# A stream stage of an RWKV block rewritten without GpSimd, and the weight splits of two paths moved to VectorE

## The chip, the cores and the metric

One NeuronCore of a Trainium2 chip runs the whole program in one launch. The metric is the device time of one execution in microseconds. Engines are named as in the profile: PE is TensorE (PEld its weight loads), DVE is VectorE, ACT is ScalarE, POOL is GpSimd, SP is SyncE, which only issues DMAs here. Each engine runs its own queue of instructions in order and waits on semaphores.

## The reference, cut to what matters

Two blocks run one after the other on 512 latent tokens and 256 context tokens of width 1024. The first has an RWKV-7 layer and a differential attention layer; the second has two layers of feed-forward halves around a mixer (Fourier, latent attention, gating, pooling). The change lies in the RWKV layer, and in one choice of engine that the second block's context path shares.

```
proj = h @ w_in                                   # r, k, v, g and the low-rank inputs lw, la
mixed = u + mu * (0.5 * (prev + nxt) - u)         # centred token shift of all but g
w_raw = w0 + tanh(lw) @ w2 ; a = sigmoid(a0 + la @ a2)        # for each direction d
decay = exp(-exp(-softplus(-w_raw) - 0.5))
kk = k * k_k ; kk = kk * rsqrt(sum(kk * kk, per head) + 1e-12)
kd = k * (1 + (a - 1) * k_a)
# scan over time, forward and backward, S is 64x64 for each of 16 heads
sa = S kk ; S = S * w - sa (kk * a)^T + v kd^T ; o = S r
y = groupnorm(o) * gn_g + gn_b + (sum r * kd * r_k) * v ; y = y * silu(g) @ w_out
```

Everything is float32 in and out. Large products run as three products of fp32r halves: high x high, high x low, low x high.

## The kernel before, in words

The 16 heads are handled in 8 pairs j of 128 features; tokens lie along the free dimension, context first (NT = 768, HALF = 384).

**Projection** (`rwkv_project`). It goes through 34 blocks of 128 output features: `l0` and `l1` (the low-rank inputs), then for each pair k, r, v and g. For a block `WStream.load` (lines 71 to 84) fetches 512 KB of weights into `wr` by an SP DMA, ScalarE copies it to `wh` rounded to fp32r (L78), and one engine subtracts to give the rest, `wl` (L81). Which engine is the parameter `lo_engines`: GpSimd for the projection and for the second block's context path, VectorE and GpSimd in turns for the latent path. TensorE then makes 24 products for each of two segments into PSUM tile `psu` (`psg` for g), ScalarE copies them to `u`, GpSimd adds the two neighbours (`sm`, L307), ScalarE scales the middle (`m`, L309), and VectorE joins both to `mx` (L314, L315). r and k stay in SBUF for the stream stage, v and g go to DRAM. Between blocks, 80 loads of modulation weights (`adaw`, three buffers) are multiplied by a small vector (`aps`).

**Stream stage** (`rwkv_streams`, `stage1(j)`). For a pair, and for each half of the tokens: squares of k, sums by head (`pc`), an inverse root in 12 small VectorE instructions (`rsqrt_cols`, lines 51 to 61, on 128x6), six products that spread it over the features (`bc`), `kap`. Then for each direction d: two LoRA products in plain float32 with 64 rows (`psw`, `psa`), tanh, a scan along the chunks (L426), a GpSimd subtraction (L427) and three exponentials (E, Ei, cs), the streams `strm` and `str` (VectorE L439 to L447, GpSimd L446, L448, L451), their way to DRAM (dS, dL), and 64x64 products `psx` masked into M (L466). After both halves, M's 96 blocks of 32x32 are regrouped through DRAM and inverted by substitution: 30 steps of a product (L485) and a sum (L486) on VectorE; products `psy` and `psz` put the inverse together.

**Scan** (`rwkv_scan`, `stage2(j)`). Groups of four chunks are prepared (`ps`, X, `psw`, `lr`, `psg`, G; masks on VectorE L607, L618, L634) and then passed through state by state (`pch`, ScalarE L683, VectorE L685 and L688). At the end of a pair the output is normalized, and GpSimd adds the bonus and multiplies by g (L729, L730).

**Order.** `stage1` is a generator: the projection runs five of its steps after each block (`s1(5)`) and lets at most one pair wait, `stage2` from the second pair on runs one step after each of its own. `C2.emit`, the context path of the second block up to its second layer, is written after the scan and its remainder (`emit2`) inside the second block. A list scheduler orders each engine's queue at build time from this order and its own costs, so that the context path's feed-forward products (`pab`, `pf` on `chi`, `clo`) fill TensorE in the scan, in the output product (`pso`) and in the differential attention (`scores`, `ptr`, `po`).

```
eng = nc.vector if self.lo[self.i % len(self.lo)] == "v" else nc.gpsimd     # line 79
eng.tensor_tensor(out=lv, in0=rv, in1=hv, op=ALU.subtract)                  # line 81
W = WStream(S, wp, ("g",), raws=2)                                          # projection
E.W = WStream(S, wp, ("g",), 512, 3, S.nc.scalar)                           # context path, in Ctx2
```

## Time and profile before

| what | us |
|---|---|
| median of 3 runs | 4411.06 |
| lowest and highest of them | 4402.58, 4414.34 |
| the profiled execution's own time | 4410.31 |
| span of its trace, first to last instruction | 4408.5 |
| VectorE busy | 2399.9 |
| GpSimd busy | 1516.9 |

The trace is one execution. A window from A to B is in microseconds from the first instruction. Busy time is the union of an engine's instructions; matmuls overlap in the pipe, so that TensorE's busy time is more than its work. PEclk is the granted share of TensorE's full clock. "X <- Y" in a view of waits means that X's engine stood idle until Y was done.

### The profile page before, as it was taken

Reading aid. Unit: us, or ns where it says so; the run is one execution under the profiler, and the core shown is the slowest. Engines: PE = TensorE matmul, PEld = TensorE weight load, DVE = VectorE, ACT = ScalarE, POOL = GpSimd, SP = SyncE. Lnnn points to the kernel's source line nnn. Section 1 sums busy time; section 2 is a strip of 40 time slices with the busy share of each in tenths; the row PEclk is TensorE's granted clock in tenths of the full one; section 3 lists DMA queues with packets and bytes.
Section 4 is the critical chain, followed back from the end, with each engine's and each line's share of the span. In section 5 each row is a group of like instructions: output and inputs, shape, how many; then the busy total and the mean of one; then the engine's idle time right before and its main releaser. Section 6 shows DMA issues by size and latency. Waiting matters only on the chain.

```text
span 4408.5 us, 70611 instructions
## 1 busy us (share of the span) xinstructions
PE 4116.0 (93%) x27478; PEld 3447.1 (78%) x27478; DVE 2399.9 (54%) x4704; ACT 1637.3 (37%) x3018; POOL 1516.9 (34%) x1200
## 2 busy tenths in 40 slices
PE   7999978899899997999898999999999999999998
PEld 5667767889768896888787888867888888867887
DVE  4677888644655435666766434554333532555434
ACT  3333333334433443444544323344222322343222
POOL 3444445355423681432333324211222222302221
PEclk9999978999999998999999999999999999999999
DMA  7775355566787663221214333311333233302332
GB/s 260 256 239 169 120 169 163 161 200 197 232 260 229 212 190 128 74 78 56 73 61 153 101 103 109 113 58 48 97 95 96 91 96 95 121 31 63 105 96 81
DMA packets 347247, 581.55 MB, mean 132 GB/s; under 512 B 96416, under 2 KB 194848, under 8 KB 345760
## 3 DMA queue, kind: packets, MB, share of 16 engines
q1 hardware_dynamic: 205984, 402.44, 28.4%
q10 hardware_dynamic: 140928, 174.58, 13.0%
q8 instruction: 217, 3.56, 0.3%
q14 instruction: 118, 0.97, 0.1%
HBM read 509.33 MB, written 67.57 MB: 131 GB/s over the span
## 4 chain that ended last, share of the span: by engine, by line
PE 70%; DVE 8%; DMA 2%; ACT 2%; issue 1%; POOL 0%; ACTq 0%; SPq 0%; DVEq 0%; POOLq 0%
PE pab L91 9%; PE pab L90 9%; PE pab L92 9%; PE pf L90 6%; PE pf L91 6%; PE pf L92 6%; PE psg L47 2%; PE pch L47 2%; PE ps L47 1%; PE psz L91 1%; PE aps L47 1%; PE pssc L47 1%; PE psz L90 1%; PE psz L92 1%; DMA adaw<-in_adaw 1%
## 5 line engine op out<-in xcount | busy, mean ns | idle before, releaser
L81 POOL TENSOR_TENSOR wl<-wr,wh 128x512 fp32r<-128x512 f32 (+3 forms) x719 | 1096.1, 1535 | 2207.3 <-ACT wh L78 1962.7
L78 ACT ACTIVATE wh<-wr 128x512 fp32r<-128x512 f32 (+3 forms) x918 | 696.5, 766 | 1476.5 <-PE pab L91 588.4
L91 PE MATMUL pab<-llo,wh 128*128 128x512 f32 (+1 forms) x1472 | 563.2, 383 | 5.2 <-DVE llo L148 5.2
L90 PE MATMUL pab<-lhi,wh 128*128 128x512 f32 (+1 forms) x1472 | 559.9, 383 | 8.2 <-ACT lhi L146 8.2
L92 PE MATMUL pab<-lhi,wl 128*128 128x512 f32 (+1 forms) x1472 | 561.7, 382 | 0.0
L90 PE MATMUL pf<-gh,wh 128*128 128x256 f32 (+1 forms) x1328 | 449.9, 342 | 31.5 <-DVE fth L1060 10.2
L91 PE MATMUL pf<-gl,wh 128*128 128x256 f32 (+1 forms) x1328 | 449.7, 340 | 3.1 <-DVE gl L158 2.8
L92 PE MATMUL pf<-gh,wl 128*128 128x256 f32 (+1 forms) x1328 | 448.6, 341 | 1.9 <-POOL wl L81 1.9
L81 DVE TENSOR_TENSOR wl<-wr,wh 128x1024 fp32r<-128x1024 f32 (+2 forms) x199 | 238.8, 1200 | 204.6 <-ACT wh L78 202.3
L90 PE MATMUL pab<-chi,wh 128*128 128x256 f32 x1056 | 310.1, 295 | 24.6 <-DVE nt L145 8.9
L90 PEld LDWEIGHTS pab<-lhi,wh 128*128 128x128 f32 x1472 | 278.7, 191 | 61.3 <-ACT lhi L146 9.5
L91 PEld LDWEIGHTS pab<-llo,wh 128*128 128x128 f32 x1472 | 280.2, 190 | 58.7 <-DVE llo L148 6.2
L92 PEld LDWEIGHTS pab<-lhi,wl 128*128 128x128 f32 x1472 | 280.3, 190 | 52.3
L92 PE MATMUL pab<-chi,wl 128*128 128x256 f32 x1056 | 307.5, 294 | 7.2 <-POOL wl L81 7.1
L90 PEld LDWEIGHTS pf<-gh,wh 128*128 128x128 f32 x1328 | 255.1, 193 | 70.5 <-ACT wh L78 15.9
L91 PE MATMUL pab<-clo,wh 128*128 128x256 f32 x1056 | 307.5, 292 | 0.0
L91 PEld LDWEIGHTS pf<-gl,wh 128*128 128x128 f32 x1328 | 257.1, 194 | 35.5 <-DVE gl L158 4.2
L92 PEld LDWEIGHTS pf<-gh,wl 128*128 128x128 f32 x1328 | 257.3, 194 | 30.3 <-POOL wl L81 2.6
L90 PEld LDWEIGHTS pab<-chi,wh 128*128 128x128 f32 x1056 | 207.6, 197 | 32.2 <-issue 15.7
L1060 DVE TENSOR_TENSOR fth<-fth,pab 128x512 f32<-128x512 f32 (+1 forms) x154 | 88.0, 572 | 265.2 <-PE pab L92 263.4
L1059 DVE SCALAR_TENSOR_TENSOR fth<-fth,pab 128x512 f32<-128x512 f32 (+1 forms) x154 | 87.7, 569 | 257.0 <-ACT fth L1058 256.8
L1034 DVE SCALAR_TENSOR_TENSOR x<-pf,lgt,x 128x512 f32<-128x512 f32 (+1 forms) x144 | 98.7, 690 | 229.4 <-PE pf L92 229.1
(508 smaller groups left out, 8944.5 us busy)
## 6 DMA issues: line engine op xcount, KB each, us to landing
adaw<-in_adaw SPq DMA_DIRECT2D x192, 512.0 KB, 5.4
wr<-in_w SPq DMA_DIRECT2D x176, 512.0 KB, 3.5
wr<-in_w ACTq DMA_DIRECT2D x344, 256.0 KB, 3.1
wr<-in_w SPq DMA_DIRECT2D x96, 384.0 KB, 3.1
wr<-in_rwin SPq DMA_DIRECT2D x32, 512.0 KB, 5.0
wr<-in_w ACTq DMA_DIRECT2D x104, 128.0 KB, 2.2
dS<-strm SPq DMA_DIRECT2D x32, 384.0 KB, 2.8
dL<-str SPq DMA_DIRECT2D x32, 384.0 KB, 3.5
```

The source lines that it names most:

```text
L47: nc.tensor.matmul(out, lhsT, rhs, start=start, stop=stop)
L78: nc.scalar.activation(out=hv, in_=rv, func=AF.Copy)
L81: eng.tensor_tensor(out=lv, in0=rv, in1=hv, op=ALU.subtract)
L90: nc.tensor.matmul(ps, whi, xhi, start=first, stop=False)
L91: nc.tensor.matmul(ps, whi, xlo, start=False, stop=False)
L92: nc.tensor.matmul(ps, wlo, xhi, start=False, stop=last)
L1034: S.nc.vector.scalar_tensor_tensor(out=E.x[:, f, sl], in0=ps[:, sl], scalar=gate[:, f : f + 1], in1=E.x[:, f, sl], op0=ALU.mult, op1=ALU.add)
L1059: nc.vector.scalar_tensor_tensor(out=th, in0=th, scalar=1.0, in1=pa, op0=ALU.add, op1=ALU.mult)
L1060: nc.vector.tensor_tensor(out=th, in0=th, in1=pb, op=ALU.mult)
```

## The change

The stream stage, the projection's sums, the readout's sums and the weight splits of two paths no longer use GpSimd.

- *Projection.* ScalarE copies `psu` to `u` already scaled by half of mu; VectorE adds the two neighbours (L310 after) and then joins `psu`, straight from PSUM, scaled by 1 - mu (L311 after): two instructions of VectorE for each segment in place of one of VectorE for each and two for the block on GpSimd and ScalarE. `wl` is made by VectorE. r and k go to DRAM like v, and `stage1(j)` loads them. There are two `u` tiles in place of three, and two buffers for `adaw` in place of three. After each block run seven steps of the stage, and no pair is waited for; `s1.ready(j)` makes sure that pair j's stage is written before its scan, and every scan step from the first pair on runs one step of it.
- *Stream stage.* The inverse root is made once for a pair (128x12), spread by a ScalarE copy (`wide`) and six transposes. The LoRA products are two fp32r products of 128 rows each: the low-rank input is kept as tiles `tw` whose upper and lower halves of partitions are its high and its low half, against weights `lh` and `ll` that stand twice. The exponential of the exclusive sum is read from E itself, shifted by one column in a tile of 65 columns per chunk, so that L427 and one exponential are gone. The products of L446, L448, L451 and L468 are VectorE's; the scaling of L444 is ScalarE's; the inverse's transposed copy (L491) is ScalarE's.
- *Readout.* The bonus, the scale and the product with g are three VectorE forms.
- *Context path.* `wl` is made by VectorE.

In the diff below, `S.ada_bufs` is 2 in the projection and 7 elsewhere, and `S1P` is 7. The diff, cut to its core:

```diff
@@ ada
+    bufs = min(bufs, S.ada_bufs)
@@ rwkv_project
-        NU = 3
+        NU = 2
-        W = WStream(S, wp, ("g",), raws=2)
+        W = WStream(S, wp, raws=2)
-            if o[0] == "k":
-                while len(pending) > 1:
-                    s1(1)
...
-                    nc.scalar.activation(out=u[:, c : c + n], in_=ps[:, :n], func=AF.Copy)
-                nc.gpsimd.tensor_tensor(out=sm, in0=u[:, 0 : NT + 1], in1=u[:, 2 : NT + 3], op=ALU.add)
-                nc.scalar.activation(out=m1, in_=u[:, 1 : NT + 2], func=AF.Identity, scale=omu[:, mc : mc + 1])
-                nc.vector.scalar_tensor_tensor(out=mx[:, 0:NCTX], in0=sm[:, 0:NCTX], scalar=hmu[:, mc : mc + 1], in1=m1[:, 0:NCTX], op0=ALU.mult, op1=ALU.add)
-                nc.vector.scalar_tensor_tensor(out=mx[:, NCTX:], in0=sm[:, NCTX + 1 :], scalar=hmu[:, mc : mc + 1], in1=m1[:, NCTX + 1 :], op0=ALU.mult, op1=ALU.add)
+                    nc.scalar.activation(out=u[:, c : c + n], in_=ps[:, :n], func=AF.Identity, scale=hmu[:, mc : mc + 1])
+                    nc.vector.tensor_tensor(out=mx[:, sl], in0=u[:, c - 1 : c - 1 + n], in1=u[:, c + 1 : c + 1 + n], op=ALU.add)
+                    nc.vector.scalar_tensor_tensor(out=mx[:, sl], in0=ps[:, :n], scalar=omu[:, mc : mc + 1], in1=mx[:, sl], op0=ALU.mult, op1=ALU.add)
...
-            s1(5)
+            s1(S1P) 
@@ stage1
+        nc.sync.dma_start(k_, S.d_rkvg[1, j])
+        nc.sync.dma_start(r_, S.d_rkvg[0, j])
...
+        rsqrt_cols(S, rc, pc[:, 0:12], 12, 1.0, 1e-12, sp)
+        nc.scalar.activation(out=wide.rearrange("p (n r) -> p n r", r=64), in_=rc.unsqueeze(2).to_broadcast([128, 12, 64]), func=AF.Copy)
...
-                    mm(nc, ps[:, :HALF], lw[ip, d, :], tw[ip, d, hs], True, True)
+                    nc.tensor.matmul(ps[:, :HALF], lh[:, 2 * d + i, :], tw[d][i][:, hs], start=True, stop=False)
+                    nc.tensor.matmul(ps[:, :HALF], ll[:, 2 * d + i, :], tw[d][i][:, hs], start=False, stop=True)
...
-                nc.gpsimd.tensor_tensor(out=th, in0=cs, in1=th, op=ALU.subtract)
-                nc.scalar.activation(out=cs, in_=th, func=AF.Exp, scale=-0.5 * CDEC)
+                E, Ex = Es[d][:, :, 1 - d : 65 - d], Es[d][:, :, d : 64 + d]
...
-                nc.gpsimd.tensor_tensor(out=kd, in0=ta, in1=kT, op=ALU.mult)
-                nc.gpsimd.tensor_tensor(out=lr[:, 1, :], in0=rT, in1=E, op=ALU.mult)
+                nc.vector.tensor_tensor(out=kd, in0=kd, in1=kT, op=ALU.mult)
+                nc.vector.tensor_tensor(out=ch(lr[:, 1, :]), in0=ch(rT), in1=E, op=ALU.mult)
@@ rwkv_scan
+            s1.ready(j)
             for _ in stage2(j):
-                if j >= 1:
-                    s1(1)
+                s1(1)
@@ Ctx2
-        E.W = WStream(S, wp, ("g",), 512, 3, S.nc.scalar)
+        E.W = WStream(S, wp, ("v",), 512, 3, S.nc.scalar)
```

Over the whole program GpSimd goes from 1205 instructions to 474, VectorE from 4706 to 5298, ScalarE from 3852 to 3845 and TensorE from 22864 to 22880 products. Up to the projection's last product TensorE's order holds 264 of the 384 products `psx` and 96 of 192 of each inverse product before, 240 and 72 after; the last modulation load of the projection stands in block 21 of the 34 before, in block 30 after.

TensorE before, in the projection, at the LoRA products of one half of a pair (`psw` and `psa`, the decay's and the rate's low-rank products, from tile `tw`):

```order
L91 MATMUL psu<-lo,wh 128x512
L47 MATMUL psx_2207<-strm 64x64 x12
L47 MATMUL psw<-tw,lw 128x384
L92 MATMUL psu<-hi,wl 128x512
L90 MATMUL psu<-hi,wh 128x512
L91 MATMUL psu<-lo,wh 128x512
```

They are one float32 product each. The same place of TensorE's queue in the changed kernel:

```order
L47 MATMUL aps<-adaw,silc 32x256 x4
L441 MATMUL psw<-tw_474,lh 128x384
L442 MATMUL psw<-tw_474,ll 128x384
L91 MATMUL psu<-lo,wh 128x512
L92 MATMUL psu<-hi,wl 128x512
L441 MATMUL psa<-tw_475,lh 128x384
L442 MATMUL psa<-tw_475,ll 128x384
```

One float32 product became two fp32r products of the same 384 columns, and both pairs of a direction stand closer together.

VectorE before, in the projection, where a pair's inversion (L485 and L486) meets the stream stage and a block's sum `mx`:

```order
L485 TENSOR_TENSOR tmp<-B 96x30
L486 TENSOR_TENSOR B<-B,tmp 96x30
L491 COPY Bt<-B 96x1024
L410 SCALAR_TENSOR_TENSOR kap<-mx,vec,bc 128x384
L423 TENSOR_SCALAR th<-th 128x384
L426 SCALAR_TENSOR_TENSOR cs<-c_smask,th 128x384
L177 COPY adas<-aps 128x256
L439 TENSOR_TENSOR strm<-kap,cs 128x384
L441 SCALAR_TENSOR_TENSOR bb<-ta,kap 128x384
L442 SCALAR_TENSOR_TENSOR strm<-bb,Ei 128x384
L444 TENSOR_SCALAR ta<-ta,kah,kao 128x384
```

No split and no neighbours' sum stands in this row. VectorE at such a place of the changed kernel, where the inversion's lines are L503 and L504:

```order
L81 TENSOR_TENSOR wl<-wr,wh 128x1024
L445 TENSOR_SCALAR th<-th 128x384
L504 TENSOR_TENSOR B<-B,tmp 96x28x3
L310 TENSOR_TENSOR mx<-u_457 128x512
L448 SCALAR_TENSOR_TENSOR cs<-c_smask,th 128x384
L184 TENSOR_TENSOR mod_68<-apt,vec 128x4x2
L503 TENSOR_TENSOR tmp<-B 96x58
L311 SCALAR_TENSOR_TENSOR mx<-psu,omu,mx 128x512
L504 TENSOR_TENSOR B<-B,tmp 96x29x2
L462 SCALAR_TENSOR_TENSOR bb<-ta,kap 128x384
L460 TENSOR_TENSOR strm<-kap,E_491 128x384
L480 TENSOR_TENSOR str_495<-r,E_491 128x384
```

The split of the projection's weights (`wl`), the neighbours' sum from `u` and the product of r stand in VectorE's row now, between steps of the inversion, and the copy `Bt` and the scaling of `ta` are gone from it.

VectorE before, in the scan, where a group of chunks is prepared (X, `lr`, G) beside the context path's feed-forward (`fth`, `gl`, `cx`):

```order
L607 TENSOR_TENSOR X_8879<-ps_8880,c_mX_6499 128x512
L1060 TENSOR_TENSOR fth<-fth,pab 128x256
L618 TENSOR_TENSOR lr_6513<-ps_8890,c_mX_6501 64x2x256
L618 TENSOR_TENSOR lr_6514<-ps_8890,c_mX_6501 64x2x256
L158 TENSOR_TENSOR gl<-fth,gh 128x256
L634 TENSOR_TENSOR G<-psg,c_mG 128x512 x2
L1059 SCALAR_TENSOR_TENSOR fth<-fth,pab 128x256
L1060 TENSOR_TENSOR fth<-fth,pab 128x256
L607 TENSOR_TENSOR X_8935<-ps_8936,c_mX_6499 128x512
```

The masks of the group follow on each other or on the feed-forward's sums. VectorE at the same place of the changed kernel:

```order
L624 TENSOR_TENSOR X_8753<-ps_8754,c_mX_6534 128x512
L81 TENSOR_TENSOR wl<-wr,wh 128x512
L635 TENSOR_TENSOR lr_6548<-ps_8764,c_mX_6536 64x2x256
L635 TENSOR_TENSOR lr_6549<-ps_8764,c_mX_6536 64x2x256
L705 COPY O<-pch_8799 64x128
L81 TENSOR_TENSOR wl<-wr,wh 128x512 x3
L1075 SCALAR_TENSOR_TENSOR fth<-fth,pab 128x256
L1076 TENSOR_TENSOR fth<-fth,pab 128x256
L651 TENSOR_TENSOR G<-psg,c_mG 128x512 x2
L158 TENSOR_TENSOR gl<-fth,gh 128x256
```

Splits of the context path's weights, one to three at a time, stand between the masks of a group, where there was none.

## Rows read from the trace of the kernel before

**Rows 1.** The page: span and busy time of each engine.

```profile
span 4408.5 us, 70611 instructions
PE 4116.0 (93%) x27478; PEld 3447.1 (78%) x27478; DVE 2399.9 (54%) x4704; ACT 1637.3 (37%) x3018; POOL 1516.9 (34%) x1200
```

**Rows 2.** Windows: stretch, length, busy us by engine (x instructions), PEclk, DMA share, GB/s.

```profile
60.00:550.00 490.00, 465.90 (x3819) 348.90 (x3817) 341.17 (x709) 169.40 (x294) 225.45 (x168) 0.95 0.62 195
550.00:875.00 325.00, 274.46 (x2820) 234.83 (x2820) 260.55 (x591) 119.07 (x259) 147.57 (x149) 0.84 0.57 163
875.00:1515.00 640.00, 612.51 (x5806) 524.47 (x5806) 338.98 (x762) 249.91 (x562) 306.52 (x293) 0.98 0.70 223
...
1720.00:2360.00 640.00, 562.73 (x3660) 508.78 (x3660) 437.59 (x979) 313.15 (x613) 219.84 (x181) 0.93 0.24 78
```

**Rows 3.** By tile, TensorE: duration ns min/median/max, first to last start.

```profile
L90 PE MATMUL psu<-hi,wh x416: 274/388/795, 45.4 to 549.6; 128*128 128x512 f32 x70, 128*128 128x256 f32 x69
...
L47 PE MATMUL psz<-Y,TT x384: 191/191/258, 280.3 to 874.6; 32*32 32x32 f32 x192
...
L47 PE MATMUL pch<-ZV,G x768: 217/275/475, 591.1 to 1468.2; 128*128 128x64 f32 x192
```

**Rows 4.** Waits of TensorE, whole run: us in total, times, longest us.

```profile
PE aps L47 <- DMA adaw<-in_adaw: 32.9, 22, 11.4
...
PE bc L47 <- DVE rc L61: 21.4, 10, 6.2
```

**Rows 5.** Timeline of TensorE around 408 us: start us, us, instruction.

```profile
408.02 0.39 PE L91 MATMUL psu<-lo,wh 128*128 128x512 f32 x1
408.25 0.39 PE L92 MATMUL psu<-hi,wl 128*128 128x512 f32 x1
...
413.08 0.91 PE L47 MATMUL psw<-tw,lw 64*128 64x384 f32 x2
413.92 0.38 PE L91 MATMUL psg<-lo,wh 128*128 128x256 f32 x1
```

**Rows 6.** Timeline of VectorE and GpSimd at 302 us.

```profile
302.40 0.40 DVE L485 TENSOR_TENSOR tmp<-B 96x238 f32<-96x238 f32 x1
302.42 2.60 POOL L81 TENSOR_TENSOR wl<-wr,wh 128x1024 fp32r<-128x1024 f32 x1 [2.92 <-ACT wh L78]
...
302.84 2.44 DVE L486 TENSOR_TENSOR B<-B,tmp 96x238 f32<-96x238 f32 x1
```

**Rows 7.** Lines of VectorE, 60 to 875 us: count, busy us, mean ns.

```profile
L485 DVE TENSOR_TENSOR tmp<-B 96x30 f32<-96x30 f32 (+14 forms) x240 | 118.0, 492 | 7.6 <-DMA B<-dM 4.1
L486 DVE TENSOR_TENSOR B<-B,tmp 96x30 f32<-96x30 f32 (+14 forms) x240 | 116.1, 484 | 3.9
```

**Rows 8.** By line, VectorE: duration ns min/median/max of four kinds of instruction.

```profile
L447 DVE TENSOR_TENSOR str<-ta,Ei x16: 540/556/1349, 130.0 to 758.4; 128x384 f32<-128x384 f32 x16
...
L158 DVE TENSOR_TENSOR gl<-fth,gh x154: 406/685/2523, 684.3 to 4360.5; 128x512 fp32r<-128x512 f32 x88, 128x256 fp32r<-128x256 f32 x66
...
L61 DVE SCALAR_TENSOR_TENSOR nrc<-rsa,nrc x69: 146/161/1221, 24.9 to 4400.0; 128x2 f32<-128x2 f32 x63, 128x4 f32<-128x4 f32 x6
```

**Rows 9.** Groups by form: the split into low halves, VectorE and GpSimd.

```profile
L81 POOL TENSOR_TENSOR wl<-wr,wh 128x512 fp32r<-128x512 f32 x406 | 530.9, 1321 | 539.6 <-ACT wh L78 425.3 <-PE pab L91 23.6 <-PE pf L91 11.5
L81 DVE TENSOR_TENSOR wl<-wr,wh 128x1024 fp32r<-128x1024 f32 x135 | 173.3, 1284 | 158.6 <-ACT wh L78 156.3
```

**Rows 10.** Windows of L81 on GpSimd alone: busy us (x instructions), PEclk.

```profile
875.00:1515.00 640.00, 231.67 (x184) 0.98 0.70 223
1720.00:2360.00 640.00, 185.69 (x149) 0.93 0.24 78
```

**Rows 11.** Waits of VectorE, whole run: us in total, times, longest us.

```profile
DVE wl L81 <- ACT wh L78: 202.3, 107, 5.6
```

**Rows 12.** Lines by form of VectorE in differential attention, 1720 to 2360 us.

```profile
L937 DVE SCALAR_TENSOR_TENSOR mx<-mx,rq 128x1 f32<-128x1 f32 x64 | 25.9, 405 | 0.7
```

**Rows 13.** The page's DMA issues: KB each, median us to landing.

```profile
adaw<-in_adaw SPq DMA_DIRECT2D x192, 512.0 KB, 5.4
```

132 lines of the change are left out of this document (70 added, 62 removed).

## The prediction

> **What bounds the kernel now.** Read the page's busy shares first, then the windows by stage, then the milestones of the tiles, then the waits. The page [rows 1] has TensorE busy for 4116 of 4408.5 us, so the first question is what TensorE still has to give. Its busy time hides two things. A matmul record is longer than its share of the pipe: two neighbours of 128x512 start 0.23 us apart and are each shown as 0.39 us [rows 5]. And in some stretches the granted clock is at the lower of its two levels. The windows [rows 2] show where: in 875 to 1515 us, where the scan runs with the context path as filler, TensorE is busy 612.5 of 640 at a clock of 0.98; in 550 to 875 us it is 274.5 of 325 at 0.84, while VectorE is busy 260.6 of 325, its highest share of any stretch. A mean of 0.84 over 325 us is about 104 us at the 1.2 GHz level, so some 52 us of full-clock time are lost there. The milestones [rows 3] say what that stretch is: the projection's last product starts at 549.6, the last piece of the stream stage at 874.6, and the scan's first state product at 591.1. So there are three regimes up to 1720 us: the projection (60 to 550), which TensorE nearly fills (465.9 of 490); the overlap (550 to 875), paced by chains through VectorE; and the rest, which TensorE fills again. Work taken off TensorE shortens the first and the third; work taken off VectorE's chains shortens the second.
>
> VectorE's time is not all work. In [rows 6] a step of the inversion takes 2.44 us because it starts 0.42 us after a GpSimd split of 2.60 us, with which it ends; the step before it, with operands of the same size, takes 0.40. The inversion's 480 instructions have a mean of 492 and 484 ns [rows 7]; taking for each size its shortest time, they would need 149 us instead of 234, so 85 us are such standing still. The same subtraction over the other 20 lines of the stream stage and the projection gives 81 more (L447, for one, has 540 as its shortest and 1349 as its longest [rows 8]), of VectorE's 602 us between 60 and 875. In the differential attention L937, one column, takes 405 ns in the mean [rows 12].
>
> **The change part by part.**
> *TensorE.* Each of the 64 LoRA products takes 0.84 us of the pipe now (413.08 to 413.92 [rows 5]). It becomes two fp32r products of 384 columns. No row has that width: above it stands 512 columns at 0.23, in proportion it is 0.17, which I take: 64 x (0.84 - 0.34) = 32 us less; by the bound 64 x 0.38 = 24. Some two thirds lie in the projection and the rest in the overlap, and what TensorE doesn't do in the overlap still counts, since the filler behind it moves up. The transposes in place of the broadcast products I leave at nothing.
> *The inverse-root chain.* TensorE waits 21.4 us in 10 waits for it [rows 4]. There are 16 such chains and will be 8, each of small VectorE instructions that stand still behind GpSimd now. I take two thirds off: -14 (bounds 0 and -21).
> *VectorE before 875 us.* Added: 34 splits of 128x1024 at 1.28 [rows 9], 43 us; 26 shifted sums in two pieces of 256 and 512 columns, at 0.41 and 0.69 as L158 [rows 8], 28 us; 96 products at 0.54 as L447, 52 us; the LoRA's and tw's splits, about 9; 34 context splits that the order now has in front of the last mask, at 0.69, 23. Gone: 32 of L444, single-input and so no longer than L447's 0.54, 15 us; half the root chains, 96 instructions of about 0.16 (L61's median is 0.166 [rows 8]), 15 us. Net +125 against up to -166 of standing still: 602 becomes about 560. That is no large relief, and the order leaves more of the stage for after the projection (five of eight stage halves and three of eight inversions are done there, against five and a half and four), so the overlap's VectorE is about as full as before. What does get shorter are the chains: the GpSimd subtraction behind the scan and the exponential behind that are gone. I take 10 us of the clock's 52 back and nothing else; bounds -40 (half of the 52, and 15 of waits) and +30 (the half pair and the inversion left over, 60 instructions of 0.31 and 20 of 0.54, on a VectorE with no room).
> *k and r through DRAM.* 16 stores and 16 loads of 384 KB. The projection covers them; in the overlap the tiles were stored long before. Nothing; at most three loads on the path, at the 5.4 us of a larger transfer [rows 13], +16.
> *Two buffers for the modulation's weights in the projection in place of three.* A load lands in 5.4 us [rows 13]; TensorE waited 32.9 us for them in the whole run [rows 4]. The order spreads the same loads over 30 of 34 projection blocks in place of 21. I take +5; bounds 0 and +20.
> *The scan (875 to 1515).* GpSimd did 184 splits there in 231.7 us [rows 10]; VectorE does nearly all at 0.69 or less (L158's 512-column median [rows 8]): about +124 on 339 us of 640, less some standing still, so two thirds busy. TensorE has filler in its order at all times, so I take +5; bounds -5 and +60 (below).
> *The readout's sums* (GpSimd before, after the scan's 48 groups) hide under the next group; nothing. *ScalarE* gives up as many instructions as it takes, at 37% busy [rows 1].
> *Differential attention (1720 to 2360).* Of 149 GpSimd splits [rows 10] all but 16 are the context path's and move: about 133, half of them 256 columns wide, 75 us at 0.69 and 0.41, on VectorE's 437.6 of 640 [rows 2]; against that L937, as small as L61, loses up to 64 x (0.405 - 0.166) = 15 us right in the chain from scores to exponential. I take -10; bounds -25 and +25. *The second block:* nothing; bounds -10 and +15, since half the latent path's splits stay on GpSimd.
> The sum: -32 - 14 - 10 + 5 + 5 - 10 = -56. The profiled run took 4410.3 us, 1.8 over its span and within 1 us of the median of the runs, 4411.06. So **4354 us**.
>
> One place of the Trainium skill speaks against the change: Perfetto Trace Analysis, § Optimizing Scalar/DVE Operations, says that with a saturated VectorE handing work to ScalarE or even GpSimd may make sense, and this change does the reverse. It adds that the two share an SBUF read port, so that moving work between them might not help; the trace agrees with that second half, as the 2.44 us step beside the 2.60 us split shows. By the first half alone VectorE's load would go up in the overlap and the time with it (the last rival below).
>
> **The rivals.**
> *The overlap gives its clock back.* If the chains through VectorE no longer stop TensorE, most of the 52 us lost to the clock come back (10 are in the sum already), and of the 24 that a clock of 0.95 costs the 490 us of the projection [rows 2] most too: 60 us more, 4294. For it: the root chain is the largest single wait before 875 us. Against: VectorE stays as full there.
> *VectorE stands still for its own splits (slower).* A split waits for ScalarE's copy of the same weights, which waits for a transfer. On GpSimd that wait held up little; on VectorE whatever is queued behind it waits too: the scan's masks (X, lr, G), from which TensorE's next group products are made, and in the attention the row maximum. VectorE's present 199 splits waited 202.3 us in 107 waits [rows 11], 1.0 us a split. About 184 + 133 more would stand for some 317 us; if a quarter reaches TensorE, 79 us take the place of the +5 and the -10 taken for the scan and the attention: 4438. It decides from about a fifth, 65 us, on. Against: the 107 waits are at places where VectorE had nothing else to do, and the order places a split where its input should be there.
> *The modulation's loads pace the projection (no change).* 80 loads go through two buffers: 40 pairs at 5.4 us and about 3 us of use and issue, and ten group ends of some 10 us: 436 us from 60 on, about the length that the projection should have. If a pair takes 9.5, the projection ends near 540, almost as before, the 46 us of its first two terms are held back there, and 4400 is left.
> *The long VectorE instructions were not GpSimd's doing (slower).* Then 602 us become 727 before 875; two fifths of the 125 added, 50 us, fall in the overlap, with some 40 of the half pair and the inversion at their present durations, on a VectorE without room: 90 us on the sum without its -10, 4454. Against: the step in [rows 6] ends with the split beside it.
>
> **How the numbers follow.** Forecast 0.48, clock back 0.20, own splits 0.16, loads 0.10, not GpSimd 0.06. About 0.3%, 13 us, is what a measurement of this kernel can tell from no change. Faster: 0.48 + 0.20 = 0.68; same: 0.10; slower: 0.16 + 0.06 = 0.22. The forecast's own bounds, taken half-way, are 4310 to 4395; the clock case reaches to about 4270, and of the slower cases the range takes the lower half, to 4430, which leaves out some 0.2.
>
> **What would show it.** In the profile after: the last psu start near 505 in place of 550; the LoRA products 0.35 us apart as a pair; the inversion's instructions with a mean near 310 ns (149 us over 480); TensorE's wait for the root chain under 8 us; VectorE's wait for the copies (split on wh) in the scan, above 100 us of which would speak for the slower rival; the clock of the overlap, above 0.92 for the faster one; aps waits above 20 us in the projection for the loads. The forecast is wrong if the scan's last state product, which starts at 1468.2 now [rows 3], starts later than 1450.

## The result and the profile after

| | kernel before | changed kernel |
|---|---|---|
| median | 4407.93 us | 4305.47 us |
| lowest to highest of 4 runs | 4402.58 to 4414.34 | 4302.32 to 4312.82 |
| ratio | | 0.9769, 95% interval 0.9752 to 0.9786 |

The change takes 102 us off; the prediction took off 56 (4354 us, range 4270 to 4430). The sign, the range and several signs in the trace came out as forecast, the size did not: the faster rival, "the overlap gives its clock back" at 4294 us, lies nearer to the measurement than the forecast does.

The page of the changed kernel, span and busy time of each engine (answers [rows 1]):

```profile
span 4300.5 us, 69854 instructions
...
PE 4046.1 (94%) x27334; PEld 3423.6 (80%) x27334; DVE 2520.6 (59%) x5296; ACT 1638.9 (38%) x3012; POOL 616.0 (14%) x469
```

VectorE has 121 us more than before, GpSimd 901 less, TensorE 70 less. VectorE is fuller, and the kernel is faster.

The mean granted clock of the one core over the whole span, in the kernel before:

```profile
core 0: 4408.5 us, clock 0.960
```

and in the changed kernel:

```profile
core 0: 4300.5 us, clock 0.966
```

The granted clock is at one of two levels, 2.4 or 1.2 GHz, so 1 minus its mean, times the span, is the time lost to the lower one: 0.040 x 4408.5 = 176 us before and 0.034 x 4300.5 = 146 us after. Of the 108 us between the two spans some 30 are clock; the other 78 are what is left for work and waits.

Windows of the changed kernel, cut where its own stages end (length, then busy us by engine for PE, PEld, DVE, ACT, POOL, then PEclk, DMA share, GB/s; projection, overlap, scan, output product, differential attention, second block; answers [rows 2]):

```profile
42.00:471.00 429.00, 420.88 (x3570) 334.10 (x3563) 308.59 (x742) 179.25 (x310) 9.97 (x11) 1.00 0.78 251
471.00:835.00 364.00, 314.27 (x3497) 284.22 (x3495) 301.30 (x760) 155.88 (x329) 37.55 (x54) 0.89 0.63 182
835.00:1406.00 571.00, 549.77 (x5172) 460.83 (x5171) 373.28 (x867) 209.38 (x478) 51.85 (x89) 0.96 0.70 224
1406.00:1623.00 217.00, 209.76 (x1552) 199.33 (x1552) 128.42 (x240) 85.00 (x150) 0.00 (x0) 0.98 0.57 186
1623.00:2250.00 627.00, 559.67 (x3700) 509.10 (x3700) 455.49 (x1114) 316.20 (x618) 72.98 (x48) 0.94 0.25 81
2250.00:4300.00 2050.00, 1970.69 (x9696) 1627.51 (x9694) 936.74 (x1519) 681.35 (x1108) 443.21 (x257) 0.98 0.29 91
```

The last four of these stages in the kernel before, cut where they end there:

```profile
875.00:1468.00 593.00, 568.37 (x5448) 484.80 (x5447) 317.69 (x718) 228.84 (x525) 273.52 (x269) 0.99 0.69 218
1468.00:1716.00 248.00, 235.59 (x1751) 221.42 (x1749) 88.97 (x155) 97.45 (x171) 141.75 (x109) 0.98 0.57 185
1716.00:2334.00 618.00, 542.99 (x3521) 490.44 (x3521) 424.90 (x953) 303.29 (x593) 207.06 (x169) 0.93 0.24 75
2334.00:4408.00 2074.00, 1993.83 (x9871) 1649.65 (x9869) 933.55 (x1503) 694.22 (x1133) 505.95 (x315) 0.98 0.29 92
```

First and last start of the three milestones, TensorE (answers [rows 3]):

```profile
L90 PE MATMUL psu<-hi,wh x416: 274/387/501, 42.4 to 470.4; 128*128 128x256 f32 x70, 128*128 128x512 f32 x69
...
L47 PE MATMUL psz<-Y,TT x384: 191/191/256, 282.7 to 834.5; 32*32 32x32 f32 x192
...
L47 PE MATMUL pch<-ZV,G x768: 217/275/476, 513.2 to 1405.7; 128*128 128x64 f32 x192
```

Read the two together with [rows 2, 3]. The projection's last product starts 79 us earlier, at 470.4, and its stretch has a clock of 1.00 where it had 0.95. The stream stage ends only 40 us earlier, at 834.5: the overlap is 364 us long instead of 325, since the order leaves more of the stage for it and TensorE does more there (3497 products for 2820), though its clock is 0.89 in place of 0.84. The scan's last state product starts 62 us earlier, at 1405.7; its clock is lower than before, 0.96 for 0.99. The other 46 us come later: the output product is 31 us shorter (217 for 248), with 199 products fewer in it, and the second block 24 us, with 175 fewer, while the attention is 9 us longer, with 179 more. What moves between these stages is the context path's filler, more of which was done earlier.

Waits of TensorE, us in total, times, longest (answers [rows 4]):

```profile
PE aps L47 <- DMA adaw<-in_adaw: 42.3, 25, 11.8
...
PE pab L92 <- DVE wl L81: 7.7, 7, 2.1
...
PE pc L47 <- ACT sq L412: 4.2, 2, 3.0
...
PE bc L425 <- ACT wide L419: 2.4, 1, 2.4
```

The wait for the inverse root, 21.4 us before, is 2.4 for the spread copy and 4.2 for the squares ahead of it. TensorE waits 7.7 us for VectorE's splits, about what it waited for GpSimd's before (7.1).

Lines of VectorE, 60 to 875 us: count, busy us, mean ns (the inversion, answers [rows 7]):

```profile
L503 DVE TENSOR_TENSOR tmp<-B 96x30 f32<-96x30 f32 (+14 forms) x240 | 80.7, 336 | 23.0 <-DMA B<-dM 19.9
L504 DVE TENSOR_TENSOR B<-B,tmp 96x30 f32<-96x30 f32 (+14 forms) x240 | 80.0, 333 | 3.2 <-DVE tmp L503 0.2
```

The inversion's instructions have 336 and 333 ns in the mean where they had 492 and 484, with the same operands: (492 - 336) x 240 + (484 - 333) x 240 = 74 us of VectorE.

Timeline of TensorE around 180 us, start and length in us (one LoRA product, answers [rows 5]):

```profile
180.50 0.34 PE L441 MATMUL psa<-tw,lh 128*128 128x384 f32 x1
180.68 0.34 PE L442 MATMUL psa<-tw,ll 128*128 128x384 f32 x1
180.85 0.39 PE L90 MATMUL psu<-hi,wh 128*128 128x512 f32 x1
```

The next product starts 0.35 us after the first of the pair, against 0.84 for the float32 product.

### The profile page after: what moved, and what is told of

It is laid out like the page before. It is cut to its first block, busy times and chain, and to the rows that moved or that the text cites. A ratio compares the mean times of both kernels' runs of the same rounds, so it can differ in the third digit from the quotient of the medians.

```text
span 4300.5 us, 69854 instructions
## 1 busy us (share of the span) xinstructions
PE 4046.1 (94%) x27334; PEld 3423.6 (80%) x27334; DVE 2520.6 (59%) x5296; ACT 1638.9 (38%) x3012; POOL 616.0 (14%) x469
## 4 chain that ended last, share of the span: by engine, by line
PE 81%; DVE 9%; DMA 6%; issue 2%; ACT 1%; SPq 0%; ACTq 0%; POOL 0%; DVEq 0%; POOLq 0%
PE pab L90 10%; PE pab L92 10%; PE pab L91 10%; PE pf L90 6%; PE pf L91 6%; PE pf L92 6%; PE aps L47 2%; DMA adaw<-in_adaw 2%; PE ps L47 2%; PE pch L47 2%; PE psg L47 2%; DVE wl L81 1%; PE psu L91 1%; PE psu L92 1%; PE psu L90 1%
## 5 line engine op out<-in xcount | busy, mean ns | idle before, releaser
L81 DVE TENSOR_TENSOR wl<-wr,wh 128x512 fp32r<-128x512 f32 (+3 forms) x727 | 594.2, 824 | 372.1 <-ACT wh L78 363.0
L81 POOL TENSOR_TENSOR wl<-wr,wh 128x1024 fp32r<-128x1024 f32 (+2 forms) x191 | 414.2, 2169 | 1907.3 <-ACT wh L78 1781.2
L92 PEld LDWEIGHTS pab<-chi,wl 128*128 128x128 f32 x1056 | 206.9, 196 | 13.5 <-DVE wl L81 10.7
```

The lines of the kernel that those rows point to most:

```text
L92: nc.tensor.matmul(ps, wlo, xhi, start=False, stop=last)
```

## The experiments

Differences in microseconds are the differences of the ratios to the kernel before on the same chip, times 4408; each ratio has an interval of about 0.002 to either side. A difference against the changed kernel is one of two such ratios, so that 9 to 14 us to either side are open in it; against the kernel before they are 6 (b_ctx) and 12 (b_dve). The scheduler orders the queues anew for every kernel, so a difference is that of the edit together with its order.

| kernel | what it is | median us | ratio and interval | against the changed kernel |
|---|---|---|---|---|
| a_lora_f32 | LoRA products in float32 | 4330.93 | 0.9822 (0.9803 to 0.9842) | +23 |
| a_proj_pool | projection's splits on GpSimd | 4332.88 | 0.9823 (0.9802 to 0.9844) | +24 |
| a_ctx_pool | context path's splits on GpSimd | 4343.85 | 0.9850 (0.9825 to 0.9876) | +36 |
| a_noise4 | extra GpSimd work beside | 4446.13 | 1.0090 (1.0067 to 1.0112) | +141 |
| a_ctx_noise | the same with a tile of its own | 4522.34 | 1.0263 (1.0238 to 1.0287) | +218 |
| a_chain | four pieces back on VectorE | 4334.81 | 0.9835 (0.9809 to 0.9861) | +29 |
| a_order | writing order of before | 4305.69 | 0.9768 (0.9749 to 0.9788) | 0 |
| a_ada3 | three buffers for the modulation | 4317.33 | 0.9798 (0.9779 to 0.9817) | +13 |
| a_nopool | the rest of GpSimd's work on VectorE | 4298.52 | 0.9751 (0.9734 to 0.9769) | -8 |
| a_best | a_nopool, one addition on ScalarE | 4291.43 | 0.9735 (0.9721 to 0.9748) | -15 |

| kernel | what it is | median us | ratio and interval | against the kernel before |
|---|---|---|---|---|
| b_ctx | context path's splits on VectorE, alone | 4389.78 | 0.9955 (0.9943 to 0.9968) | -20 |
| b_dve | GpSimd's work of the change's stages on VectorE, nothing rewritten | 4364.42 | 0.9894 (0.9867 to 0.9920) | -47 |

**LoRA products.**

```diff
-  nc.tensor.matmul(ps[:, :HALF], lh[:, 2 * d + i, :], tw[d][i][:, hs], start=True, stop=False)
-  nc.tensor.matmul(ps[:, :HALF], ll[:, 2 * d + i, :], tw[d][i][:, hs], start=False, stop=True)
+  mm(nc, ps[:, :HALF], lw[:, 2 * d + i, :], tw[d][i][:, hs].bitcast(F32), True, True)
```

> The changed kernel with one part undone: each LoRA product is one plain float32 product again (the full weights against the same tile of high and low halves), without the split of the weights. Theory A (TensorE sets the pace before the stream stage's end, so that work on it counts in full, as the prediction's first term had it): 64 products of 0.84 us in place of 64 pairs of about 0.42 us by the trace of after: 20 to 32 us longer, 4325 to 4338 us, two thirds of it before the projection's last product. Theory B (TensorE has room there, since it still loses some 67 us in the projection to waits): under 8 us longer, 4305 to 4314 us.

Measured +23: theory A. The undone product has 128 rows and not the 64 of the kernel before, so that it is not quite the old one. Its order differs too: the stream stage ends at 804 us, 30 us before the changed kernel's, with less filler ahead of its end.

**The splits, each path alone.**

```diff
-  W = WStream(S, wp, raws=2)                            # projection
+  W = WStream(S, wp, ("g",), raws=2)                    # a_proj_pool
...
-  E.W = WStream(S, wp, ("v",), 512, 3, S.nc.scalar)     # context path
+  E.W = WStream(S, wp, ("g",), 512, 3, S.nc.scalar)     # a_ctx_pool
```

> The changed kernel with the projection's 34 weight splits back on GpSimd, 2.4 us each there against 1.28 on VectorE. Theory A (standing still beside GpSimd is what stretched VectorE's instructions before the end of the stream stage): the inversion's mean goes from 335 up to 380 ns or more, VectorE's saving of 43 us is eaten, and the time is 5 to 20 us longer, 4310 to 4325 us. Theory B (VectorE's load counts, not the neighbour): the mean stays near 335 ns and the time is 5 to 15 us shorter, 4290 to 4300 us.

Measured +24, somewhat above theory A. Though VectorE has 43 us less to do, the time grows, and between 60 and 875 us VectorE is busy as long as in the changed kernel (622 and 623 us). The inversion's mean went to 363 and 371 ns only, so A's mechanism is there and smaller than A's 380. Windows of a_proj_pool, projection and overlap:

```profile
43.00:497.00 454.00, 437.99 (x3732) 346.59 (x3733) 333.93 (x734) 183.62 (x319) 89.35 (x45) 0.97 0.76 241
497.00:834.00 337.00, 284.25 (x3117) 257.87 (x3114) 278.14 (x709) 145.65 (x305) 36.09 (x46) 0.87 0.63 182
```

The stream stage ends where it does in the changed kernel, but TensorE has done 218 products fewer by then (6849 against 7067); at the changed scan's pace, 571 us for 5172, that is an estimated 24 us. The projection loses 0.03 x 454 = 14 us to the clock, against nothing in the changed kernel. No wait of TensorE's in the projection is put down to GpSimd's split, so that the slower split itself does not show as the cause.

> The changed kernel with the context path's weight splits back on GpSimd. Theory A (the prediction: VectorE's own work and the standing still about balance in scan and attention): within 8 us of the changed kernel, 4298 to 4314 us. Theory B (GpSimd beside VectorE is what cost the time, in scan, output product and attention too): 15 to 40 us longer, 4320 to 4345 us, most of it after the stream stage's end, with the one-column instruction of the attention (L953) back near 0.40 us. Theory C (VectorE waits for its own splits): 10 us or more shorter, under 4295 us.

Measured +36: theory B, against the prediction. Windows of this kernel, overlap, scan and output product:

```profile
476.00:843.00 367.00, 307.62 (x3333) 279.38 (x3332) 290.95 (x677) 150.23 (x316) 118.34 (x111) 0.84 0.59 172
843.00:1415.00 572.00, 547.00 (x5192) 464.50 (x5189) 312.35 (x715) 211.03 (x481) 244.48 (x248) 0.97 0.69 221
1415.00:1657.00 242.00, 230.21 (x1702) 213.06 (x1701) 94.87 (x159) 91.33 (x159) 135.12 (x102) 0.99 0.57 186
```

Groups of VectorE, the inversion's product (60 to 875 us) and the attention's one-column instruction:

```profile
L503 DVE TENSOR_TENSOR tmp<-B 96x30 f32<-96x30 f32 (+14 forms) x240 | 91.5, 381 | 18.6 <-DMA B<-dM 15.6
...
L953 DVE SCALAR_TENSOR_TENSOR mx<-mx,rq 128x1 f32<-128x1 f32 x64 | 26.6, 416 | 0.7
```

The scan is as long as in the changed kernel (572 and 571 us), although GpSimd is busy 244 us of it. The overlap, where 61 of these splits lie, is back at a clock of 0.84: 0.16 x 367 = 59 us lost there against 0.11 x 364 = 40. It is hardly longer, but TensorE does 164 products fewer in it (3333 for 3497), and the output product, with 150 more, takes 242 us against 217: the context path's filler that fell behind is made up for there and in the second block. The one-column instruction is at 416 ns again (271 in the changed kernel), but the attention itself is no longer. VectorE gives up 494 splits, some 320 us of its time in the changed kernel (390 of them at 706 ns, 104 at 444), and is busy only 136 us less (2384 against 2521): more than half of the relief goes in standing still.

The same edit of the context path alone, made on the kernel before:

> The kernel before with one thing alone: the context path's weight splits are VectorE's in place of GpSimd's. The prediction had this at about nothing (5 us in the scan, -10 in the attention, VectorE no fuller in sum before 875 us). Theory A (GpSimd beside VectorE costs in the overlap and the output product, whatever the rest is): 20 to 45 us shorter than before, 4365 to 4390 us, and at least half of it gone by the end of the output product. Theory B (it only pays once the other GpSimd work is gone too): within 13 us of before, 4396 to 4422 us.

Measured -20 by the ratio, the near edge of theory A, and -17 by the medians, between the theories; and not where A had it: the output product ends at 1713 us against 1716, and the rest is gained behind it. So the edit is worth about half as much while the other GpSimd work is still there, and the overlap, at a clock of 0.83, gets nothing back from it.

**GpSimd's leaving alone.** In the kernel before, each `nc.gpsimd` of the projection, the stream stage and the readout became `nc.vector`, and both paths' splits went to VectorE.

> The kernel before with one thing alone: every instruction of the projection, the stream stage, the readout and the context path's splits that GpSimd had is VectorE's, with the same operands, and nothing is rewritten. Theory A (taking GpSimd away is what gave the clock and the waits back): 40 to 75 us shorter than before, 4333 to 4368 us, with the inversion's mean near 335 ns and a clock near 1.0 in the projection. Theory B (without the rewriting VectorE is too full, since the neighbours' sum and the subtraction behind the scan come on top): within 15 us of before, or longer, 4393 us and above.

Measured -47: theory A by the time, but its clock in the projection is not there. Windows of projection and overlap:

```profile
43.00:529.00 486.00, 475.81 (x3882) 358.67 (x3882) 352.96 (x893) 183.97 (x319) 10.21 (x9) 0.95 0.65 205
529.00:878.00 349.00, 298.97 (x3066) 259.34 (x3065) 279.37 (x729) 129.40 (x280) 33.95 (x50) 0.84 0.57 162
```

Lines of VectorE, the inversion, 60 to 875 us:

```profile
L485 DVE TENSOR_TENSOR tmp<-B 96x30 f32<-96x30 f32 (+14 forms) x240 | 78.3, 326 | 11.7 <-DMA B<-dM 9.4
L486 DVE TENSOR_TENSOR B<-B,tmp 96x30 f32<-96x30 f32 (+14 forms) x240 | 79.6, 332 | 2.4
```

The inversion has the short instructions of the changed kernel, 326 and 332 ns, with the operands and the code of before. TensorE's waits at the broadcast products, ten with 21.4 us before, are one of 7.3 us, put down to the inversion ahead of the chain, although the chains are still 16. The chain's last instruction, which took up to 2.36 us before, takes no more than 0.31 here: standing still beside GpSimd was most of these waits, as far as these rows show. The clock has stayed at 0.95 and 0.84. So nearly half of the 102 us comes from GpSimd's leaving without any rewriting, and almost none of that as clock (0.961 over the span, 0.960 before). The overlap is no shorter than before, so short instructions alone did not quicken it.

**GpSimd beside, with nothing else moved.** VectorE keeps the split; GpSimd subtracts once more, into the tile of loaded weights that VectorE has just read, where nothing reads the result.

```diff
   eng.tensor_tensor(out=lv, in0=rv, in1=hv, op=ALU.subtract)
+  if self.cap == 512:                                     # the context path
+      nc.gpsimd.tensor_tensor(out=rv, in0=rv, in1=hv.bitcast(F32), op=ALU.subtract)
```

> The changed kernel, in which GpSimd subtracts once more for each of the context path's splits, into the tile of the loaded weights that VectorE has just read; nothing reads what it writes but the next load of that buffer waits for it. TensorE still waits for VectorE's split, and the order keeps the context path at its places (480 of its products in the overlap, 492 in the changed kernel). Theory A (the 38 us of the context path's splits on GpSimd are VectorE standing still beside it): 20 to 60 us longer than the changed kernel, 4325 to 4365 us, as VectorE keeps its own splits too. Theory B (they are the late split itself): within 12 us, 4297 to 4317 us.

Measured +141: theory A's direction, far outside its size. The 494 extra instructions are useless, TensorE reads nothing of theirs, and they cost 0.29 us each. Of the 145 us between the two traces 37 lie in the overlap, 63 in the output product and 34 in the attention. A first form, with an extra tile for the result, had cost still more:

> The changed kernel, in which GpSimd makes each of the context path's weight splits a second time into a tile that nothing reads, beside the one of VectorE that TensorE waits for. Theory A (the 38 us that the context path's splits cost on GpSimd are VectorE standing still beside it): most of them come back, 4325 to 4350 us, and the one-column instruction of the attention (L956 there) is near 0.41 us again. Theory B (they are TensorE's filler being late, since a split takes GpSimd about twice as long and waits in its queue): under 12 us, 4303 to 4317 us, though L956 is long again.

That one proves less: with the extra 2 KB of SBUF the order starts the context path only near the stream stage's end, with 48 of its first feed-forward products (`pab`) in the overlap where the changed kernel has 492. The overlap's clock falls to 0.72, which goes with the filler that is gone, but the run mixes two causes. In a_noise4 the order has 480. Timeline of VectorE and GpSimd around 700 us in a_noise4:

```profile
699.07 1.42 POOL L83 TENSOR_TENSOR wr<-wr,wh 128x512 f32<-128x512 f32 x1
699.29 1.42 DVE L447 TENSOR_SCALAR th<-th 128x384 f32<-128x384 f32 x1
...
702.52 0.39 DVE L505 TENSOR_TENSOR tmp<-B 96x238 f32<-96x238 f32 x1
...
707.15 1.46 POOL L83 TENSOR_TENSOR wr<-wr,wh 128x512 f32<-128x512 f32 x1 [2.07 <-issue]
707.40 1.47 DVE L505 TENSOR_TENSOR tmp<-B 96x240 f32<-96x240 f32 x1
```

The inversion's product of 96x240 takes 1.47 us: it starts 0.25 us after a GpSimd instruction of 1.46 us and ends 0.26 us after it. Its neighbour of 96x238, with GpSimd at rest, takes 0.39. The single-input addition `th`, with 0.355 us in the changed kernel, takes 1.42 beside GpSimd. The group of VectorE's splits of 128x512 in a_noise4:

```profile
L81 DVE TENSOR_TENSOR wl<-wr,wh 128x512 fp32r<-128x512 f32 x406 | 373.7, 931 | 89.3 <-ACT wh L78 84.8 <-ACT lr L646 2.2 <-PE pab L94 0.4
```

and in the changed kernel:

```profile
L81 DVE TENSOR_TENSOR wl<-wr,wh 128x512 fp32r<-128x512 f32 x406 | 282.7, 706 | 119.8 <-ACT wh L78 116.1 <-PE pf L92 1.1 <-PE pab L92 0.4
```

931 ns against 706: 91 us over 406 instructions in this group alone. A second effect, that the next load of the tile waits for GpSimd, was not separated from this, and TensorE's wait for VectorE's splits of the context path grew from 7.7 to 27.5 us; so the 141 us are an upper bound of what the standing still alone costs in this kernel.

**The rewriting.** Four things go back to VectorE:

```diff
-  rsqrt_cols(S, rc, pc[:, 0:12], 12, 1.0, 1e-12, sp)
+  for q6 in (slice(0, 6), slice(6, 12)):
+      rsqrt_cols(S, rc[:, q6], pc[:, q6], 6, 1.0, 1e-12, sp)
...
+  nc.vector.tensor_tensor(out=th, in0=cs, in1=th, op=ALU.subtract)
...
+  nc.scalar.activation(out=cs, in_=th, func=AF.Exp, scale=-0.5 * CDEC)
...
-  nc.scalar.activation(out=kd, in_=ta, func=AF.Identity, scale=kah[...], bias=kao[...])
+  nc.vector.tensor_scalar(out=kd, in0=ta, scalar1=kah[...], scalar2=kao[...], op0=ALU.mult, op1=ALU.add)
...
-  nc.vector.tensor_tensor(out=ch(kst), in0=ch(kap), in1=Ex, op=ALU.mult)
+  nc.vector.tensor_tensor(out=kst, in0=kap, in1=cs, op=ALU.mult)
...
-  nc.scalar.activation(out=Bt[L], in_=B[L].rearrange("p s t -> p t s"), func=AF.Copy)
+  nc.vector.tensor_copy(Bt[L], B[L].rearrange("p s t -> p t s"))
```

> The changed kernel with the four things put back on VectorE that the rewriting took off it in the stream stage, and nothing on GpSimd: two chains of 128x6 for the inverse root in place of one of 128x12, the scaling of ta, the transposed copy of the inverse, and the subtraction behind the scan with its third exponential on ScalarE. That is 96 x 0.16 + 32 x 0.36 + 8 x 1.4 + 32 x 0.55 = some 55 us of VectorE before the end of the stream stage. Theory A (what is left of the gain beyond GpSimd's leaving, the LoRA products and the two buffers, some 20 us, is VectorE's shorter chains, which keep TensorE's clock up near the projection's end): 12 to 30 us longer, 4317 to 4335 us, with 10 us or more lost to the clock before the projection's last product. Theory B (VectorE has room for them, 12 to 30% of it idle there, once GpSimd is gone): within 8 us, 4298 to 4314 us.

Measured +29, theory A's size, but not its place. Windows of a_chain, projection and overlap:

```profile
41.00:455.00 414.00, 407.90 (x3329) 323.92 (x3322) 300.69 (x742) 156.16 (x280) 9.86 (x11) 0.99 0.76 245
455.00:902.00 447.00, 371.89 (x4006) 333.88 (x4004) 374.43 (x980) 167.16 (x368) 43.38 (x62) 0.83 0.59 172
```

The projection keeps its clock (0.99) and ends 16 us earlier than in the changed kernel, since less of the stage gets into it. The overlap pays: 447 us at 0.83, that is 0.17 x 447 = 76 us lost to the clock, against 40. VectorE is busy 374 us of these 447. So the 55 us on VectorE's chains cost about half of themselves, in the overlap, and much of that as clock. GpSimd has no part in this: VectorE's own load counts in the overlap, too.

**Order and buffers.**

```diff
-S1P = 7
+S1P = 5
...
         for i, o in enumerate(order):
+            if o[0] == "k":
+                while len(pending) > 1:
+                    s1(1)
```

> The changed kernel with the writing order of before in the projection: five steps of the stream stage after each block in place of seven, and at most one pair waiting at a block of k. Theory A (the 22 us of clock that the projection got back are due to the steps being spread more evenly through it): 10 to 25 us longer, 4315 to 4330 us, with 30 us or more at the lower clock before the projection's last product. Theory B (the order of these steps is not what did it): within 8 us of the changed kernel, 4298 to 4314 us.

No difference: theory B. The writing order around the projection's blocks costs nothing that these runs can tell.

```diff
-        S.ada_bufs = 2
+        S.ada_bufs = 3
```

> The changed kernel with three buffers for the modulation's weights in the projection, as before, so that their loads and small products run further ahead. The prediction's term for the two buffers was 5 us: 4300 us. Theory A (the wait for these loads has a price): 3 to 8 us shorter, 4297 to 4303 us. Theory B (with two buffers the small products last through the projection and fill TensorE's gaps there, which keeps its clock up): 8 to 20 us longer, 4313 to 4325 us, with more time at the lower clock before the projection's last product. Between the two nothing is shown.

Measured +13, just clear of its interval of 11: by the time theory B, by the place not. Windows of a_ada3, projection and overlap:

```profile
42.00:462.00 420.00, 416.02 (x3526) 332.07 (x3526) 305.44 (x723) 179.58 (x309) 10.33 (x11) 1.00 0.76 251
462.00:849.00 387.00, 329.49 (x3576) 299.11 (x3576) 309.41 (x790) 159.59 (x339) 40.65 (x56) 0.87 0.61 178
```

The projection keeps a clock of 1.00 and ends 9 us earlier; the overlap is 23 us longer, at 0.87. With two buffers the modulation's products last to 427 us in place of 361, so that the projection ends later, and the overlap is shorter by more than that. Neither kernel loses clock in the projection; why the overlap gains is not settled.

**What is left on GpSimd.** In a_nopool the latent path's and the attention's splits, the low halves of the norms (all in the two-instruction form, without GpSimd and its ScalarE copy) and of the gated values, the scaled identities, the rotation's product and the pooling sums are VectorE's.

> The changed kernel with nearly all that GpSimd still does moved to VectorE with the same operands: the latent path's and the attention's weight splits that went to it in turn, the low halves of the norms, the scaled identities of the scan, the rotation's product, the pooling sums. Theory A (GpSimd beside VectorE is a cost wherever VectorE has two SBUF operands): 10 to 40 us shorter, 4265 to 4295 us, and the mean of the low halves gl (L158), 1293 ns in the second block, falls to about 690. Theory B (the second block is TensorE's, so that nothing there reaches the end): within 10 us, 4295 to 4315 us. Theory C (VectorE now is the one that is late for the weights): longer than 4315 us.

Measured -8, theory B's interval and not clear of the noise. Group of the low halves gl of 128x512 in a_nopool:

```profile
L158 DVE TENSOR_TENSOR gl<-fth,gh 128x512 fp32r<-128x512 f32 x88 | 60.3, 685 | 1.5 <-ACT gh L157 0.8
```

and in the changed kernel:

```profile
L158 DVE TENSOR_TENSOR gl<-fth,gh 128x512 fp32r<-128x512 f32 x88 | 117.3, 1332 | 32.4 <-ACT gh L157 31.9
```

The standing still is gone (1332 to 685 ns, 57 us in this group), and hardly any of it reaches the end. One reason is that TensorE, busy 1971 of 2050 us at 0.98 in the changed kernel's second block, leaves little to gain there; this is argued. Another is a loss ahead of it. Window of a_nopool's overlap:

```profile
470.00:859.00 389.00, 329.98 (x3579) 298.72 (x3581) 324.57 (x840) 158.53 (x332) 3.41 (x12) 0.86 0.60 176
```

It is 25 us longer than the changed kernel's, with more on VectorE (325 us for 301), and the output product ends 23 us later, at 1646; what follows is 23 us shorter. So what is gained behind the output product is, in this one trace, about what is lost ahead of its end.

```diff
-  nc.vector.tensor_scalar(out=th, in0=th, scalar1=1.0, scalar2=None, op0=ALU.add)
+  nc.scalar.activation(out=th, in_=th, func=AF.Identity, bias=1.0)      # on top of a_nopool
```

> The changed kernel with nearly all of GpSimd's remaining work on VectorE, as in a_nopool, and the addition behind the first tanh (L445), 32 instructions of 0.354 us, on ScalarE. Theory A (what is taken off VectorE in the stream stage comes back at about half, as the 55 us put there cost 29): 3 to 8 us shorter than a_nopool, 4290 to 4296 us, with less time lost to the clock in the overlap. Theory B (it is the length of a chain that counts, and ScalarE's addition is as long as VectorE's): within 3 us of a_nopool, 4296 to 4302 us.

Measured 4291.43 us, 7 below a_nopool and within theory A's band, the lowest median of this study: ratio 0.9735, whose interval ends below the point where the changed kernel's begins. The intervals of a_best and a_nopool overlap, so that theory B, within 3 us, is not excluded. The clock half of theory A is not confirmed: the profiled run of this kernel lost more to it in the overlap (0.18 x 399 = 72 us) than that of a_nopool (0.14 x 389 = 54), from one trace of each.

## Why the prediction was right and wrong

**LoRA products, -32: right within the noise.** The pair takes 0.35 us, as taken, and undoing it costs 23 us, against bounds of 24 and 32.

**Root chain, -14: the size right, the reason half.** The wait fell from 21.4 to 6.6 us. But b_dve has it down to 7.3 with all 16 chains in place, and a_chain, with the 16 put back, to 0.8. It was GpSimd that held these small instructions, and halving them was hardly needed for it.

**Clock, -10: the term that was mis-sized.** 30 us came back. The prediction read the 0.84 of the overlap and took 10 of its 52 us; 12 came (52 to 40). It had named the 24 us that a clock of 0.95 costs the projection, and put them into the rival alone: they came back nearly whole (PEclk 1.00). In the scan the clock fell from 0.99 to 0.96, so that some 10 to 20 us went the other way. What gave the projection its clock is open. a_proj_pool, with GpSimd's splits back, has 0.97 there, so they had a part in it; but b_dve, with GpSimd gone and nothing rewritten, keeps 0.95; a_lora_f32, a_chain, a_order and a_ada3, each without one part of the rewriting, keep 0.98 to 1.00. No run undid, among others, the sums read straight from PSUM, the way of r and k through DRAM and the readout's new form.

**VectorE before 875 us, 602 becoming 560 and 10 us gained: a wrong step.** It weighed sums: 125 us added against up to 166 of standing still, "about as full as before". As full it was, though not 560: VectorE is busy 309 + 301 = 610 us in projection and overlap, where [rows 2] has 602. The inversion's 335 ns for 310 are 12 us of the difference, and some 66 of the context path's splits lie in the overlap, 41 us, where 34 with 23 were counted. What failed is the conclusion that a sum that stays level gains little. An instruction that stands still holds up whatever waits for it, and a sum does not tell it from work: a_proj_pool takes 43 us of work off VectorE, leaves its busy time the same and is 24 us longer. The load counts as well, as a_chain shows (55 us more work, GpSimd no part in it, 29 us longer). That the length of each link of a chain sets the overlap's pace is argued and not shown: b_dve's inversion is as short as the changed kernel's, and its overlap stays at 0.84.

**Two buffers, +5: wrong sign, by a little more than the noise.** A third buffer put back costs 13. TensorE's wait for these loads in the projection is 4.7 us, so the rival of the loads was false too.

**Scan +5 and attention -10: wrong place.** The prediction priced the context path's splits where most of them lie [rows 10]. The scan had room either way (571 and 572 us), as forecast; and the wait of VectorE for ScalarE's copies, which grew from 202 to 363 us, hardly reached TensorE:

```profile
DVE wl L81 <- ACT wh L78: 363.0, 255, 10.0
```

In the changed kernel's scan it is 42 us, under the 100 that was to speak for the slower rival, and TensorE waits some 9 us for VectorE's splits in the whole run. But these splits cost 36 us on GpSimd, in the overlap's clock and the output product, places where the prediction had them at 23 us of added VectorE work or not at all. In the changed kernel's own stages GpSimd has no split left in the scan (835 to 1406 us) and 16 in the attention (1623 to 2250), as foreseen. The attention's stretch is 9 us longer and not 10 shorter, with 179 products more in it, so that its own gain can't be read from it. Its one-column instruction got shorter, by about half of what was allowed for (answers [rows 12]):

```profile
L953 DVE SCALAR_TENSOR_TENSOR mx<-mx,rq 128x1 f32<-128x1 f32 x64 | 17.3, 271 | 0.5
```

That is 64 x (0.405 - 0.271) = 9 us of the up to 15 that the prediction gave it. It took 0.166 us from [rows 8] for this, where the row has 161 ns; that changes nothing.

**The signs.** The last psu was to start near 505 and starts at 470: some 22 us of that are the clock; the rest goes with the part of the stage that was left for later, which no run sizes. The inversion was to have 310 ns and has 335. GpSimd still makes the scaled identities beside it, which is about half of that: with nothing on GpSimd (a_nopool) it has 323. The root chain (under 8), the loads (under 20) and the last state product (before 1450) lie where they were to lie, and the overlap's clock of 0.89 is short of the 0.92 that was to speak for the faster rival.

**The rivals.** "Not GpSimd's doing" is refuted by b_dve's inversion and by a_noise4. "The overlap gives its clock back" came half true: 30 of its 70 us of clock, in the projection more than in the overlap. With the terms as measured by undoing (LoRA 23, projection's splits 24, context's splits 36, chains 29, buffers 13) the sum is 125, above the 102: the parts share what they gain, and the terms are not to be added. That the range holds the result is owed to the clock rival, for which it was drawn out to 4270: the forecast's own bounds, taken half-way, ended at 4310, and the measurement lies below them.

The page Perfetto Trace Analysis of the Trainium skill, § Optimizing Scalar/DVE Operations, was weighed in the prediction: hand work from a saturated VectorE to GpSimd. Here the reverse gained, with VectorE up from 54% to 59% of the span; the second half, that with the shared port such a move might not help, agrees with the runs, in which VectorE's instructions stand still beside GpSimd's (0.39 to 1.47 us in the timeline of a_noise4).

## What to carry to other kernels

Before moving work to GpSimd to relieve VectorE, compare the mean of VectorE's instructions with the shortest of the same shape: if they differ, part of the relief will be paid for by VectorE standing still. Price a change of engine where TensorE waits on chains (here a clock of 0.84 and VectorE 80% busy), not only where most of the moved instructions lie: in the scan here, which TensorE fills, the same standing still left the length as it was (572 and 571 us). A useless instruction on the neighbour engine, with the order held the same, bounds its price from above.

## What the runs showed of the hardware that was not expected

Not only instructions with two SBUF inputs stand still beside GpSimd. The addition `th`, with a single input, took 1.42 us instead of 0.355 in the timeline above, and a_ctx_pool has the same once. An instruction with one operand in PSUM does not: G, masked from PSUM, never took more than 0.69 us, though 60 of its 96 ran beside a GpSimd instruction of more than 0.5 us (counted in the trace). Rows of a_ctx_pool, duration ns min/median/max, first and last start:

```profile
L651 DVE TENSOR_TENSOR G<-psg,c_mG x96: 662/684/693, 514.2 to 1400.9; 128x512 f32<-128x512 f32 x96
...
L445 DVE TENSOR_SCALAR th<-th x32: 342/360/1415, 117.5 to 700.1; 128x384 f32<-128x384 f32 x32
```

The Trainium skill, SBUF — State Buffer, § Who interferes with whom, states this: two SBUF inputs contend with a GpSimd instruction that reads SBUF, a one-input operation in a two-port mode contends with GpSimd, the pair of ports being an exclusive lock, and one SBUF input outside those modes does not. The rows agree with the first case (`tmp`, 0.39 and 1.47 us) and the last (G); that `th` ran in a two-port mode is in no row, only that it stood still.

What the neighbour takes need not all come back at the end: in a_noise4 VectorE's busy time grew by 219 us (2740 against 2521), 0.44 us for each GpSimd instruction, and the kernel by 141.
